# On-chip rotary tables, paired tiles and weights cast in flight in an eight-core encoder kernel

## The chip, the cores and the metric

The kernel runs on all eight cores of one Trainium2 chip. Each core computes two of the sixteen sequences and holds all weights; no core talks to another. The time is the device time of the slowest core in microseconds (us). A core has five engines that run their own instruction streams: TensorE (PE; its weight loads are listed as PEld), VectorE (DVE), ScalarE (ACT), GpSimd (POOL) and SyncE (SP), which here does nothing but issue DMA transfers. Some executions fall into a slower state of the chip, with the cores of one die or of both at a lower clock (in one run of e1, cores 0 to 3 had 0.875 to 0.881 and the time was 2512.55 us). Only fast runs are compared below.

## The reference, cut to what matters

```python
n1 = rmsnorm(h, g_mix)
q, k, v, u, gates = split(n1 @ w_in)
q, k = apply_rope(rmsnorm(q, g_q), cos, sin), apply_rope(rmsnorm(k, g_k), cos, sin)
a = gqa_block_attention(q, k, v) @ w_attn_up          # every key, both directions
p = (multiscale_pool(u) @ pool_w * pool_scale) @ w_pool_up
h = h + (g_a * a + g_p * p) @ w_out                   # sigmoid gates g_a, g_p
n2, mn = rmsnorm(h, g_cross), rmsnorm(mem, g_mem)     # 256 memory tokens a sequence
h = h + softmax((n2 @ w_xq) @ (mn @ w_xk).T / 16) @ (mn @ w_xv) @ w_xo
h = h + square(relu(rmsnorm(h, g_ffn) @ w_ff1)) @ w_ff2
return rmsnorm(h, g_final)                            # x is 16 x 2048 x 1024, f32
```

The kernel works in eight blocks of 512 tokens a core. Before block 0 it makes keys and values of the first sequence (four tiles), and beside the attention of block 0 it folds the memory weights: w_xq with the memory keys, the memory values with w_xo.

## The kernel before

The program is not written in the order in which it runs. Python code builds a graph of operations, and an order-maker, a list scheduler in the same file, walks it with a cost for each operation, chooses an engine where several could do it, gives buffer slots, and writes one fixed sequence for each engine. Its costs are constants in the file:

```python
DMA_BW = 318.0; BACKLOG = 6000.0; DMA_LAT = 2000.0; DMA_ISSUE = 420.0
# a DMA may be placed when its queue is less than BACKLOG behind
if o.dma is not None:
    r = max(r, dma_free - BACKLOG)
...
def pool_t(n):                       # ns of a GpSimd tensor_tensor
    return 150.0 + n * 1.9
def TT(fn, R, W):                    # either engine; the order-maker chooses
    return G.op((("dve", dve_t(512)), ("pool", pool_t(512))), fn, R, W, port=True)
```

A weight is read as f32 in two halves of 128x1024 (on its first one to three uses) and cast to bf16 by one of three engines; from its last such use a bf16 copy goes to a scratch tensor, from which later uses load it. Both stores and loads go through SyncE.

```python
SIZES = dict(W=(10, 2048, BF16), M2=(10, 1024, F32), M1=(24, 512, F32), S1=(70, 512, BF16), KV=(4, 2048, BF16))
wst = nc.dram_tensor("wst", [NU, 2, 128, 1024], F32, kind="ExternalInput").ap()
...
for hf in range(2):                                  # in weight()
    r = V(f"raw{name}{i}{hf}", "M2")
    load(lambda r=r: ap(r), wst[uid, hf], 524288, [r])
    copy_any(lambda w=w, hf=hf: ap(w)[:, hf * 1024:(hf + 1) * 1024], lambda r=r: ap(r), 1024, ...,
             engs=("pool", "act", "dve") if scale is None else ("act", "dve"))
if keep and n == late:
    store(wsc[uid], lambda w=w: ap(w), 524288, [(w, 0), (w, 1)], [dram(("wsc", key))])
...
def rope_tables(tb):                                 # cos and sin of a tile: two loads
    for i in range(2):
        c = V("cs", "M1")
        load(lambda c=c: ap(c), rope_d[tb, i], 262144, [c], early=30000.0)
```

The softmax here doesn't subtract the row's maximum and nothing guards it: scores larger than these inputs give would overflow.

Of the kernel before, what the change touches and what calls it, by code (L numbers as in the profile page):

```python
# [65 lines left out]
DMA_BW = 318.0  # L66
BACKLOG = 6000.0
DMA_LAT = 2000.0
DMA_ISSUE = 420.0
ALT_BIAS = 300.0  # L70
# [132 lines left out]
def schedule(G, pools, horizon, pe_ahead):  # L203
# [75 lines left out]
    while n_left:  # L279
# [4 lines left out]
        for level in range(2):  # L284
            for e in engines:
# [5 lines left out]
                for U, i, o in lst:  # L291
# [11 lines left out]
                    if best is not None and r > best[0] + 400.0 and r > s_min + 400.0:  # L303
                        n += 1
                        continue
# [14 lines left out]
                if best is None or c[0] < best[0]:  # L320
                    best = (c[0], e, c[3])
# [37 lines left out]
        if o.mms is not None:  # L359
            if o.mms[0]["mode"] != last_mode:  # L360
                start += SWITCH
            last_mode = o.mms[-1]["mode"]
            d = o.dur
            o.start, end = start, start + d
            o.finish = end + PE_TAIL
        elif e == "sp":
            end = start + DMA_ISSUE
            dma_free = max(dma_free, end) + o.dma / DMA_BW
            o.start, o.finish = start, dma_free + DMA_LAT
            d = DMA_ISSUE  # L370
        else:
            d = dict(o.engs)[e]
            o.start, end = start, start + d
            o.finish = end
            if e == "pool" or o.port and e == "dve":
                port_free = end
# [30 lines left out]
def emit(nc, stack, order):  # L407
# [33 lines left out]
    for o in allops:  # L441
# [12 lines left out]
        if o.dma is not None:  # L454
            kn = known[e]
            idle = [s for s, c in dcount.items() if kn.get(("d", s), 0) >= 16 * c]
            s = min(idle, key=lambda s: dcount[s]) if idle else len(dcount)
# [16 lines left out]
    dsem = {s: stack.enter_context(nc.semaphore(f"d_{s}")) for s in dcount}  # L474
# [48 lines left out]
def build_core(info=None):  # L523
    nc = bass.Bass("TRN2", target_bir_lowering=False, dynamic_dma_scratch_size=256)
    xT = nc.dram_tensor("xT", [2, 4, 8, 128, 512], F32, kind="ExternalInput").ap()
    memT = nc.dram_tensor("memT", [8, 128, 512], F32, kind="ExternalInput").ap()
    wst = nc.dram_tensor("wst", [NU, 2, 128, 1024], F32, kind="ExternalInput").ap()
    vec_d = nc.dram_tensor("vec", [128, 64], F32, kind="ExternalInput").ap()
    rope_d = nc.dram_tensor("rope", [4, 2, 128, 512], F32, kind="ExternalInput").ap()
    band_d = nc.dram_tensor("band", [2, 128, 864], F32, kind="ExternalInput").ap()  # L530
# [3 lines left out]
    n1d = nc.dram_tensor("n1d", [2, 4, 8, 128, 512], BF16).ap()  # L534
    pdd = nc.dram_tensor("pdd", [2, 4, 4, 128, 512], BF16).ap()
# [3 lines left out]
    with st:  # L539
# [3 lines left out]
        SIZES = dict(W=(10, 2048, BF16), M2=(10, 1024, F32), M1=(24, 512, F32), S1=(70, 512, BF16), KV=(4, 2048, BF16))  # L543
# [9 lines left out]
        poolw = sb("poolw_sb", [128, 512], BF16)  # L553

# [6 lines left out]
        def ap(v):  # L561
            if v.pool == "E":
                return ps[:, v.slot, :]
# [3 lines left out]

        def b16(v):
            return ap(v).bitcast(BF16)

        CONST = {k: Val(k, None) for k in ("vec", "nbg", "ones", "bd", "band", "poolw")}
# [14 lines left out]
        def pool_t(n):  # L586
            return 150.0 + n * 1.9
# [25 lines left out]

        def store(dst, src, nbytes, R, W):
# [21 lines left out]
        def constants():  # L636
            load(lambda: vec[:], vec_d, 32768, [CONST["vec"]])
            for i in range(2):
                b = V("bandraw", "M2")
                load(lambda b=b: ap(b)[:, 0:864], band_d[i], 442368, [b])  # L640
                copy_any(lambda i=i: band[:].rearrange("p a n -> p (a n)")[:, i * 864:(i + 1) * 864],
                         lambda b=b: ap(b)[:, 0:864], 864, [b], [(CONST["band"], i)], psum=False, rate=2.0)
            b = V("pwraw", "M2")
            load(lambda b=b: ap(b)[:, 0:512], poolw_d, 262144, [b])
            copy_any(lambda: poolw[:], lambda b=b: ap(b)[:, 0:512], 512, [b], [CONST["poolw"]], psum=False, rate=2.0)
# [10 lines left out]
        def weight(name, i, keep=True, scale=None):  # L656
# [4 lines left out]
            if key in UNITS and n <= late:  # L661
                uid = UNITS[key]
                for hf in range(2):
                    r = V(f"raw{name}{i}{hf}", "M2")
                    load(lambda r=r: ap(r), wst[uid, hf], 524288, [r])
                    sc = None if scale is None else (lambda hf=hf: vec[:, scale + 2 * i + hf:scale + 2 * i + hf + 1])
                    copy_any(lambda w=w, hf=hf: ap(w)[:, hf * 1024:(hf + 1) * 1024], lambda r=r: ap(r), 1024,
                             [r] + ([CONST["vec"]] if scale is not None else []), [(w, hf)], psum=False, scale=sc, rate=2.0,
                             engs=("pool", "act", "dve") if scale is None else ("act", "dve"))
# [43 lines left out]
        def scaled(h, g, r, name="n"):  # L713
            n = V(name, "S1")
# [7 lines left out]
        def rope_tables(tb):  # L722
            cs = []
            for i in range(2):
                c = V("cs", "M1")
                load(lambda c=c: ap(c), rope_d[tb, i], 262144, [c], early=30000.0)
# [28 lines left out]
        def pool_tile(s, tb):  # L755
            mmsg = []
            for g in range(4):
# [3 lines left out]
                for i, kt in enumerate(kts):  # L761
# [7 lines left out]
                                  i == 0, i == len(kts) - 1, [(u, 0), (u, 1), (CONST["band"], 0), (CONST["band"], 1)],  # L769
                                  n=max(hi - lo, 230)))  # L770
                mmsg.append((g, b, mms))
            for g, b, mms in mmsg:
                PE(mms, [b])
                p = V("pd", "S1")
                copy_any(lambda p=p: ap(p), lambda b=b: ap(b), 512, [b], [p], engs=("act", "dve"))
                if (s, tb) == (0, 0):
                    PD0.append(p)
                else:
                    store(pdd[s, tb, g], lambda p=p: ap(p), 131072, [p], [dram(("pd", s, tb, g))])

        def tile_steps(s, tb, W):
# [3 lines left out]
            def norm():  # L785
# [11 lines left out]
                st_["n"] = [scaled(xs[kc], C_GMIX + kc, r, "n1") for kc in range(8)]  # L797
# [35 lines left out]
            def keep():  # L833
# [3 lines left out]
                for kc in range(8):  # L837
                    n = st_["n"][kc]
                    store(n1d[s, tb, kc], lambda n=n: ap(n), 131072, [n], [dram(("n1", s, tb, kc))])
# [12 lines left out]
        def memory_steps():  # L852
            m = {}

            def norm():
# [10 lines left out]
                m["n"] = [scaled(xs[kc], C_GMEM + kc, r, "mn") for kc in range(8)]  # L866
# [14 lines left out]
            def fold_a(h, ch):  # L881
                def f():
                    if ch == 0:
                        m["wq"] = weight("XQ", h, keep=False)
                        m["A"] = [V("A0", "W"), V("A1", "W")]
                    w, At = m["wq"], m["A"]
                    b = V("fa", "D")
                    PE([mm(lambda: ap(b), wsl(w, dt * 1024 + ch * 128), lambda dt=dt: ap(m[("XK", 2 * h + dt)]), dt == 0, dt == 1,
                           [(w, dt), m[("XK", 2 * h + dt)]]) for dt in range(2)], [b])
                    for s in range(2):  # L890
                        copy_any(lambda s=s: ap(At[s]).rearrange("p (a k d) -> p a k d", a=2, d=128)[:, :, ch, :],
                                 lambda s=s: ap(b)[:, s * 256:(s + 1) * 256].rearrange("p (a d) -> p a d", d=128), 256,
                                 [b, CONST["vec"]], [(At[s], ch)], scale=lambda: vec[:, C_GCROSS + ch:C_GCROSS + ch + 1],
                                 engs=("act", "dve"))
                    if ch == 7:
                        for s in range(2):
                            store(wsc[SCRATCH[(f"A{s}", h)]], lambda s=s, At=At: ap(At[s]), 524288,
                                  [(At[s], k) for k in range(8)], [dram(("wsc", (f"A{s}", h)))])
# [154 lines left out]
        def query_steps(s, tb):  # L1053
            d_ = {}

            def query(c):
                def f():
                    if c == 0:
                        if (s, tb) not in N1:
                            N1[(s, tb)] = []  # L1060
                            for kc in range(8):
                                n = V("n1g", "S1")
                                load(lambda n=n: ap(n), n1d[s, tb, kc], 131072, [n], R=[dram(("n1", s, tb, kc))], early=15000.0)
                                N1[(s, tb)].append(n)
# [38 lines left out]
        def chain_steps(s, tb, lead, nxt):  # L1103
# [3 lines left out]
            def up_step(j):  # L1107
                def f():
                    if j == 0:
                        c_["pd"] = PD0 if (s, tb) == (0, 0) else []  # L1110
                        for g in range(4 if (s, tb) != (0, 0) else 0):
                            p = V("pdl", "S1")
# [382 lines left out]
```

## Time and profile before

| | |
|---|---|
| time, median of 4 runs | 2254.18 us (2251.19 to 2256.78) |
| cores in the profiled run | 2242.3 to 2253.9 us, granted clock 0.986 to 0.990 |
| PE busy on the slowest core | 2140.6 us, 95% |
| a repeating block of 512 tokens | 246 us |

These are lines of the page's part on DMA queues (packets, MB, share of the time of 16 engines) and of its part on DMA issues (count, KB each, median us from issue to landing), for the kernel before.

```profile
q1 hardware_dynamic: 156096, 440.60, 60.7%
...
HBM read 376.57 MB, written 63.96 MB: 195 GB/s over the span
...
M_p<-wst SPq DMA_DIRECT2D x228, 512.0 KB, 9.8
...
M_p<-rope SPq DMA_DIRECT2D x32, 256.0 KB, 10.7
n1d<-S_p SPq DMA_DIRECT2D x56, 128.0 KB, 9.1
```

One queue carries everything. The 228 half weights, 32 rotary tables and 56 small stores are the rows that the change touches.

### The profile page before, as it was taken

To read this page: it belongs to the slowest core of one execution; us is meant where nothing else is said; L and a number is where in the kernel's file an instruction comes from. 1 tells how busy PE (TensorE), PEld (TensorE's weight loads), DVE (VectorE), ACT (ScalarE), POOL (GpSimd) and SP (SyncE) were. 2 spreads that over 40 slices of the span, in tenths; PEclk is the share of its full clock that TensorE was granted. 3 is DMA by queue.
4 is the path that set the end of the run, shared out by engine and by line. 5 is a ranking of instruction groups with operands and counts; after the bars stand their busy time and mean duration, and the time that the engine had idled before them with its cause. 6 is when DMAs were issued, how large, how long until landed. Compare 5 with 4: busy or idle time off the path is not lost.

```text
span 2253.9 us, 33704 instructions; the slowest of 8 cores (2242.3 to 2253.9 us)
## 1 busy us (share of the span) xinstructions
PE 2140.6 (95%) x10758; PEld 900.0 (40%) x10758; DVE 1471.4 (65%) x1793; ACT 1481.2 (66%) x1875; POOL 368.5 (16%) x273
## 2 busy tenths in 40 slices
PE   6788999988999999999999999999999999999997
PEld 3423333333444434444434443444434443444443
DVE  4688876667876687666774578557774687456502
ACT  6678777747786477853788368854786368835550
POOL 0112321124221241101110021002110122000100
PEclk9999999999999999999999999999999999999998
DMA  9957995989587992946633463435533463336342
GB/s 284 287 189 244 299 306 185 286 277 314 199 275 267 284 306 101 299 153 197 211 113 122 151 223 104 139 124 191 174 117 117 168 215 113 123 128 226 127 145 75
DMA packets 156267, 442.75 MB, mean 196 GB/s; under 512 B 17472, under 2 KB 38976, under 8 KB 156096
## 3 DMA queue, kind: packets, MB, share of 16 engines
q1 hardware_dynamic: 156096, 440.60, 60.7%
q8 instruction: 91, 1.49, 0.3%
q14 instruction: 80, 0.66, 0.1%
HBM read 376.57 MB, written 63.96 MB: 195 GB/s over the span
## 4 chain that ended last, share of the span: by engine, by line
PE 81%; DMA 6%; ACT 4%; DVE 4%; issue 3%; SPq 1%; POOL 0%; DVEq 0%; ACTq 0%; POOLq 0%
PE ps L603 81%; DMA M_p<-wst 3%; ACT M_p L1014 2%; DMA wsc<-W_p 1%; SPq L611 1%; DMA outT<-M_p 1%; SPq L615 1%; DMA M_p<-xT 1%; DVE M_p L1270 0%; DMA vec_sb<-vec 0%; ACT M_p L1241 0%; DVE M_p L1025 0%; ACT M_p L709 0%; DVE S_p L715 0%; ACT W_p L623 0%
## 5 line engine op out<-in xcount | busy, mean ns | idle before, releaser
L603 PE MATMUL ps<-S_p,W_p 128*128 128x512 bf16 x7680 | 1731.9, 381 | 33.1 <-DVE S_p L715 7.7
L603 PEld LDWEIGHTS ps<-S_p,W_p 128*128 128x128 bf16 x7680 | 733.7, 98 | 996.2 <-issue 160.3
L1014 ACT ACTIVATE M_p<-ps 128x2048 bf16<-128x2048 f32 x256 | 479.5, 1873 | 220.3 <-PE ps L603 215.9
L1025 DVE TENSOR_TENSOR M_p<-M_p 128x1024 f32<-128x1024 f32 x224 | 284.5, 1270 | 162.2 <-ACT M_p L1014 158.0
L1026 DVE TENSOR_TENSOR M_p<-M_p 128x1024 f32<-128x1024 f32 x224 | 309.6, 1382 | 17.4 <-DVE M_p L1025 0.9
L698 POOL TENSOR_TENSOR M_p<-M_p 128x512 f32<-128x512 f32 x67 | 101.3, 1512 | 806.3 <-ACT M_p L689 710.4
L689 ACT ACTIVATE M_p<-M_p 128x512 f32<-128x512 f32 x216 | 134.1, 625 | 137.2 <-DVE M_p L1222 47.0
L626 POOL CAST W_p<-M_p 128x1024 bf16<-128x1024 f32 x92 | 115.1, 1256 | 493.8 <-PE ps L603 291.8
L1241 ACT ACTIVATE M_p<-ps 128x512 f32<-128x512 f32 x256 | 151.6, 592 | 46.7 <-PE ps L603 45.2
L1257 DVE TENSOR_TENSOR M_p<-ps,M_p 128x512 f32<-128x512 f32 x64 | 44.2, 691 | 208.3 <-PE ps L603 208.3
L603 PE MATMUL ps<-S_p,KV_p 64*128 64x512 bf16 x1024 | 157.1, 385 | 15.4 <-ACT M_p L1014 14.8
L603 PE MATMUL ps<-M_p,KV_p 128*64 128x512 bf16 x1024 | 137.0, 389 | 16.6 <-ACT M_p L1014 12.3
L1245 ACT ACTIVATE S_p<-M_p 128x512 bf16<-128x512 f32 x220 | 138.6, 630 | 20.4
L623 ACT ACTIVATE W_p<-M_p 128x1024 bf16<-128x1024 f32 x71 | 74.4, 1051 | 108.1 <-PE ps L603 88.3
L1092 ACT ACTIVATE M_p<-ps,nbg 128x512 f32<-128x512 f32 x128 | 87.1, 685 | 58.7 <-PE ps L603 57.9
L603 PE MATMUL ps<-W_p,S_p 128*128 128x256 bf16 (+2 forms) x576 | 96.1, 318 | 4.0 <-ACT W_p L623 1.8
L603 PEld LDWEIGHTS ps<-M_p,KV_p 128*64 128x64 bf16 x1024 | 49.3, 110 | 96.7 <-issue 72.2
L626 DVE CAST W_p<-M_p 128x1024 bf16<-128x1024 f32 x61 | 42.7, 716 | 65.4 <-PE ps L603 29.2
L603 PEld LDWEIGHTS ps<-S_p,KV_p 64*128 64x128 bf16 x1024 | 29.6, 94 | 121.4 <-issue 121.3
L603 PE MATMUL ps<-S_p,ones_bf 128*128 128x512 bf16 x166 | 56.5, 403 | 19.0 <-ACT S_p L689 11.6
L603 PEld LDWEIGHTS ps<-W_p,S_p 128*128 128x128 bf16 x576 | 55.1, 100 | 43.6 <-issue 21.3
L1095 ACT ACTIVATE M_p<-M_p 128x1024 f32<-128x1024 f32 x64 | 67.5, 1055 | 4.1
(76 smaller groups left out, 1486.7 us busy)
## 6 DMA issues: line engine op xcount, KB each, us to landing
W_p<-wsc SPq DMA_DIRECT2D x383, 512.0 KB, 4.3
M_p<-wst SPq DMA_DIRECT2D x228, 512.0 KB, 9.8
wsc<-W_p SPq DMA_DIRECT2D x69, 512.0 KB, 9.3
M_p<-xT SPq DMA_DIRECT2D x128, 256.0 KB, 10.6
outT<-M_p SPq DMA_DIRECT2D x64, 256.0 KB, 4.7
M_p<-rope SPq DMA_DIRECT2D x32, 256.0 KB, 10.7
n1d<-S_p SPq DMA_DIRECT2D x56, 128.0 KB, 9.1
S_p<-n1d SPq DMA_DIRECT2D x56, 128.0 KB, 5.6
```

The lines of the kernel that those rows point to most:

```text
L603: return e.matmul(out(), lhsT=lhsT(), rhs=rhs(), start=start, stop=stop, skip_group_check=True, **kw)
L623: return e.activation(out=dst(), in_=src(), func=AF.Copy)
L626: return e.tensor_copy(out=dst(), in_=src())
L689: A(lambda e: e.activation(out=ap(sq), in_=src(), func=AF.Square), 512, False, R, [sq])
L698: TT(lambda e: e.tensor_tensor(out=ap(out), in0=ap(acc), in1=ap(sq), op=ALU.add), [acc, sq], [out])
L1014: A(lambda e: e.activation(out=b16(P).rearrange("p (a n) -> p a n", n=512), in_=ps[:, 0:4, :], func=AF.Exp, scale=0.125), 2048, True, S, [P])
L1025: D(lambda e: e.tensor_tensor(out=ap(acc), in0=ap(acc), in1=lo(), op=ALU.add), 1024, [P, acc], [acc], port=True)
L1026: D(lambda e: e.tensor_tensor(out=ap(acc), in0=ap(acc), in1=hi(), op=ALU.add), 1024, [P, acc], [acc], port=True)
L1092: A(lambda e, b=b, i=i: e.activation(out=ap(Et)[:, i * 512:(i + 1) * 512], in_=ap(b), func=AF.Exp, bias=nbg[:, i * 8 + j:i * 8 + j + 1], s ...
L1095: A(lambda e: e.activation(out=ap(Et), in_=ap(Et), func=AF.Ln, bias=1.0, scale=1.0), 1024, False, [(Et, 0), (Et, 1)], [(Et, 0), (Et, 1)])
L1241: A(lambda e: e.activation(out=ap(rl), in_=ap(b), func=AF.Relu), 512, True, [b], [rl])
L1245: e.activation(out=ap(H), in_=ap(rl), func=AF.Square))
```

## The change

Its intent is to free engines, SyncE and bandwidth in the crowded front of the run. Weights come as one transfer of 1 MB, cast to bf16 on the way and issued by GpSimd; rotary tables are products of a small table in SBUF; n1 and pooled tiles travel in pairs; folding writes 512 columns at a time. With it come new constants of the order-maker. The core of the diff, cut where marked:

```diff
-DMA_BW = 318.0
-BACKLOG = 6000.0
+DMA_BW = 385.0
+DMA_FIX = 200.0
+BACKLOG = 5000.0
+SW_ISSUE = 620.0
+SW_LAT = 3000.0
...                       (SyncE may be placed up to 1600 ns later, not 400, and is preferred when urgent)
-    wst = nc.dram_tensor("wst", [NU, 2, 128, 1024], F32, kind="ExternalInput").ap()
+    wst = nc.dram_tensor("wst", [NU, 128, 2048], F32, kind="ExternalInput").ap()
...
-M1=(24, 512, F32), S1=(70, 512, BF16)
+M1=(32, 512, F32), S1=(50, 512, BF16)
...
         def pool_t(n):
-            return 150.0 + n * 1.9
+            return 270.0 + n * 1.95
...
+        def load_cast(dst, src, nbytes, W):
+            return G.op((("pool", SW_ISSUE + nbytes / DMA_BW + SW_LAT),), lambda e: e.dma_start(out=dst(), in_=src), (), W,
+                        dma=nbytes)
...                                                  (weight)
-                for hf in range(2):
+                if scale is None:
+                    load_cast(lambda w=w: ap(w), wst[uid], 1048576, [(w, 0), (w, 1)])
+                for hf in range(2) if scale is not None else ():
...                                                  (rope_tables)
-                load(lambda c=c: ap(c), rope_d[tb, i], 262144, [c], early=30000.0)
+                TT(lambda e, c=c, i=i: e.tensor_tensor(
+                    out=ap(c).rearrange("p (r c) -> p r c", c=64),
+                    in0=rope[:, i * 32 + tb * 8:i * 32 + tb * 8 + 8].unsqueeze(2).to_broadcast([128, 8, 64]),
+                    in1=rope[:, 64 + i * 64:128 + i * 64].unsqueeze(1).to_broadcast([128, 8, 64]), op=ALU.mult),
...                                                  (n1; the pooled tiles likewise)
-                for kc in range(8):
-                    store(n1d[s, tb, kc], lambda n=n: ap(n), 131072, [n], [dram(("n1", s, tb, kc))])
+                for k2 in range(4):
+                    store(n1d[s, tb, k2], lambda v=v: b16(v), 262144, [(v, 0), (v, 1)], [dram(("n1", s, tb, k2))])
...                                                  (fold_a: four products of 256 columns, one eviction of 512)
-                    for s in range(2):
-                        copy_any(..., 256, [b, CONST["vec"]], [(At[s], ch)], scale=..C_GCROSS.., engs=("act", "dve"))
+                    copy_any(..., 512, [b], [(At[s], c2)], engs=("act", "dve"))
...
-                    rounded(j, None)
+                    rounded(j, C_GCROSS)
```

## The prediction

> **What bounds the kernel now.** I read the per-core list first: cores 2242 to 2254 us, both dies at clock 0.987 to 0.988, so the fast state and no odd core. Then the page's busy line, then a table of busy time by stage whose cuts I chose at the borders that the timeline shows: the four key/value tiles (to 118 us), the folding of the memory weights beside attention block 0 (to 257), the first block (to 560), blocks 1 and 2 with the late tiles (to 1150), three repeating blocks, the end. Columns of the table: stretch, length, busy time of PE, PEld, DVE, ACT, POOL with instruction counts, granted clock, DMA share, GB/s.
>
> ```profile
> PE 2140.6 (95%) x10758; PEld 900.0 (40%) x10758; DVE 1471.4 (65%) x1793; ACT 1481.2 (66%) x1875; POOL 368.5 (16%) x273
> ...
> 0.00:118.00 118.00, 85.20 (x484) 44.16 (x484) 65.91 (x119) 77.56 (x132) 12.85 (x15) 0.92 0.99 285
> 118.00:190.00 72.00, 57.06 (x283) 19.95 (x285) 61.64 (x79) 57.09 (x69) 15.85 (x12) 0.94 0.63 207
> 190.00:257.00 67.00, 59.88 (x307) 21.24 (x304) 56.81 (x63) 51.04 (x55) 11.62 (x9) 0.97 0.79 254
> 257.00:560.00 303.00, 282.49 (x1370) 116.06 (x1369) 220.21 (x266) 218.00 (x266) 86.92 (x66) 0.98 0.88 276
> 560.00:1150.00 590.00, 579.30 (x3031) 251.07 (x3031) 424.85 (x522) 404.48 (x515) 117.75 (x89) 1.00 0.70 225
> 1150.00:1396.00 246.00, 242.94 (x1216) 99.48 (x1210) 160.43 (x184) 162.44 (x198) 33.17 (x22) 1.00 0.45 150
> ```
>
> The reader is to see two kernels in one. From 1150 us on a block takes 246 us, PE is busy for 242.9 of them and DMA for 45%: nothing that feeds PE matters there. PE's idle time sits at the front: 118 - 85.2 = 32.8 us, then 14.9, 7.1, 20.5 and 10.7. If PE idled throughout at the rate of a repeating block (3.1 of 246), the first 1150 us would hold 14 us of idle; they hold 86. About 72 us is thus the whole prize, and some 18 of it is the start, before the first projection matmul at 18.3 us. Each early stage has its own limit: DMA to 118 us (share 0.99), DVE and ACT from 118 to 190 (61.6 and 57.1 of 72), DMA and casts mixed after that.
>
> The timeline around 80 to 101 us shows the front's worst hole (start, duration, engine, line, instruction, in brackets the idle time before and what ended it):
>
> ```profile
> 79.29 7.42 SPq L615 DMA_DIRECT2D n1d<-S_p  x8
> ...
> 86.75 1.40 SPq L611 DMA_DIRECT2D M_p<-wst  x2
> ...
> 98.72 1.06 ACT L623 ACTIVATE W_p<-M_p 128x1024 bf16<-128x1024 f32 x1 [7.22 <-DMA M_p<-wst]
> ...
> 100.89 1.18 PE L603 MATMUL ps<-S_p,bd_bf 128*128 128x512 bf16 x2 [5.28 <-ACT S_p L732]
> ```
>
> Eight small stores hold the SP queue for 7.4 us, the weight load behind them lands at 98.6, its cast follows, and PE has idled 5.3 us.
>
> **What the Trainium skill says.** (1) "DMA: Bandwidth & Descriptors", section "SWDGE vs HWDGE vs iDMA": a DMA that changes the type has to come from GpSimd, whose cores write the descriptors in software. The kernel before has no such DMA, so no row shows the cost. (2) Same page, "Issuing engines are not separate DMA queues": transfers from all engines share the same 16 DMA engines, so a second issuer saves issue time, not bandwidth. The trace agrees with the premise: with one issuer the DMA share is already 0.99 at 285 GB/s. (3) "SBUF — State Buffer", section "Who interferes with whom": a DVE instruction in a 2-port mode locks GpSimd out of its SBUF port, and descriptor writing waits. The trace has candidates (DVE casts 1024 f32 in 716 ns, hardly more than the 691 of its undisturbed sum of two 512 wide operands, so a fast mode) but they are short, and 61 of them disappear. (4) DMA page, "Rules for kernel authors": small transfers pay mostly overhead, coalesce. Here a 128 KB n1 store lands in 9.1 us and a 512 KB scratch load in 4.3, but the former run in the crowded part, so this is weak support.
>
> **The change part by part.**
>
> ```profile
> L626 POOL CAST W_p<-M_p 128x1024 bf16<-128x1024 f32 x92 | 115.1, 1256 | 493.8 <-PE ps L603 291.8 <-DMA M_p<-wst 181.7 <-DMA wsc<-W_p 20.1
> ...
> L623 ACT ACTIVATE W_p<-M_p 128x1024 bf16<-128x1024 f32 x71 | 74.4, 1051 | 108.1 <-PE ps L603 88.3 <-DMA M_p<-wst 18.1 <-DMA wsc<-W_p 1.7
> ...
> L626 DVE CAST W_p<-M_p 128x1024 bf16<-128x1024 f32 x61 | 42.7, 716 | 65.4 <-PE ps L603 29.2 <-DMA M_p<-wst 28.8 <-DMA wsc<-W_p 7.2
> ...
> L627 DVE TENSOR_SCALAR W_p<-ps,vec_sb 128x256 bf16<-128x256 f32 x33 | 14.7, 478 | 3.9 <-PE ps L603 2.0 <-DMA wsc<-W_p 1.3
> ...
> L624 ACT ACTIVATE W_p<-ps,vec_sb 128x256 bf16<-128x256 f32 x31 | 13.3, 476 | 3.6 <-DVE W_p L627 1.5 <-DMA wsc<-W_p 1.2 <-PE ps L603 0.4
> ```
>
> Casts: 92 + 71 + 61 = 224 go, worth 115 us of POOL, 74 of ACT, 43 of DVE (four scaled halves stay). None lies after 1150 us. In their place POOL issues 112 transfers of 1 MB; at an assumed 1 us each (my estimate, near an SP issue of 0.3 to 0.9 us) POOL keeps about the same load as before. HBM reads stay the same, only the SBUF side is halved. SP issues fall from 1084 to about 740.
>
> Rotary tables: 32 loads of 256 KB go (8.4 MB, 1.9% of all bytes); ten of them are issued before 118 us, 2.6 MB, at 285 GB/s 9 us of DMA time where DMA is the limit. Added: 32 products of 128x512 f32, about 0.69 us on DVE (that form, undisturbed) or 1.3 to 1.5 on POOL: 22 to 45 us over the whole run, 7 us of it in the first stage, hidden beside DMA.
>
> Pairing: n1 and pooled stores and loads fall from 168 to 84, same bytes. It halves holes like that at 79 us, 4 us each at most, and overlaps with the gain from weights leaving the SP queue.
>
> Folding: 64 evictions of 128x256 (28.0 us of DVE and ACT) become 32 of 128x512, at 684 (DVE) or 601 ns (ACT) about 20.6 us: 7.4 saved. But 64 matmuls of 512 columns become 128 of 256. In the tiles 16 such took 2.34 us (146 ns each), 16 of 512 columns 3.63 (227 each): 64 x (2 x 146 - 227) = 4 us more PE time. The gain g_cross moves into the rounding of h: 18 casts of 832 ns leave POOL for ACT or DVE (706 or 600 ns), some 16 us spread over all blocks, hidden.
>
> The sum by stage. To 118 us: 9 us less DMA time; the first matmul cannot start much sooner (vec, x and three weight units must land), so I give it 8. From 118 to 257: ACT and DVE lose 11.6 + 4.3 us of casts and 7.4 of evictions, 23 in all, 11.6 each when shared; 2 us of table products and 4 of PE time come back, and attention's chain of score, exponential, sum does not shrink: I give it 8 of the 22 us idle. From 257 to 560: 1 MB of tables at 276 GB/s is 3.8 us, and 56 us of casts leave ACT and DVE; of 20.5 us idle I give it 7. To 1150: 2. After: 0. Sum 25, less 1 for dearer rounding between stages: 24, so 2255.9 - 24 = 2232 us.
>
> **The rivals.** (a) The buffer takes the place of the cast. Before, the raw half sat ready in its own buffer, and when a weight slot came free only a cast of about 1 us lay between; now a slot must be free before the load starts, and loads take 7 to 12 us to land in the front. The chain of waits already has the scratch store as the freeing event (5.5 us at 178, 7.9 at 237). Against it: ten slots, and a weight is used up in about 3.6 us (16 matmuls), so 36 us of lead, against some 10 + 4 + 9 for load, use and store. If it binds, it eats the gain of the middle stages: 2250 to 2275. (b) POOL becomes a gate: its instructions run in order, so a transfer stands behind a sum that waits for ACT. POOL is 11 to 29% busy in the front, which speaks against it; 0 to +15 us. (c) DMA stays the limit and the casts were hidden anyway: then only the removed table bytes count, some 9 + 4 us, 2243. (d) All of it works and PE idles as in a repeating block except for the start: 72 - 18 = 54 us, 2202. That is the floor of what I believe.
>
> **Range and chances.** Over 2% faster needs less than 2211, 45 of the 54 us in (d): 0.15. Slower by over 2% needs 2301; no row offers 45 us of new wait unless (a) and (b) meet: 0.05. Range 2204 to 2258, (d) at its low end and a mild (a) at the other.
>
> **What would show each step.** The repeating blocks should still take 246 us; if they shrink, my reading of the bound is wrong. No casts of 128x1024 f32 into W_p but four, no table loads, SP issues near 740. PE idle to the end of the tiles near 25 instead of 33, in the folding stage near 14 instead of 22, in the first block near 14 instead of 20. Rival (a) would show as matmuls waiting directly on weight DMA with the issue waiting on a scratch store, (b) as POOL's issues late behind its sums, (c) as the same DMA share of 0.99 and an unchanged length of the middle stages. What would make it wrong most likely: cast transfers that run faster or slower per byte than plain ones, which nothing here shows, or a changed order of instructions that moves idle time by itself.

## The result, and the profile after

The changed kernel takes 2277.76 us, the median of four runs (2272.62 to 2310.91, the last of them slow). The kernel before, on the same chip, takes 2254.18. The ratio of fast runs is 1.0097, with a 95% interval from 1.0073 to 1.0122. (Ratios here and below are the mean time of one kernel's fast runs over the mean of the other's fast runs of the same rounds, so they are not quite the ratio of the medians.) The change is within 2%, on the slow side, and outside my range.

The page of the changed kernel, its slowest core:

```profile
PE 2145.9 (94%) x10822; PEld 907.9 (40%) x10822; DVE 1409.2 (62%) x1702; ACT 1428.8 (63%) x1819; POOL 339.5 (15%) x307
...
q1 hardware_dynamic: 106848, 313.70, 41.2%
q0 software_dynamic: 16416, 59.30, 16.9%
...
L627 POOL DMA_DIRECT2D W_p<-wst x112 | 60.8, 544 | 519.6 <-PE ps L615 424.5
...
W_p<-wst POOLq DMA_DIRECT2D x112, 512.0 KB, 8.7
```

The parts do what was meant. DVE and ACT each lose over 50 us of work, a second queue carries 112 cast transfers (the page counts the 59 MB that they write), and POOL spends 544 ns on each. A cast transfer lands 8.7 us after its issue. PE has 64 more matmuls and 5 us more work. The table by stage, for the slowest core (5), has the columns of the one in the prediction (its cuts are points in time, so the two kernels need not be at the same piece of work there):

```profile
0.00:118.00 118.00, 80.86 (x480) 43.41 (x480) 70.75 (x118) 66.28 (x126) 23.99 (x30) 0.94 0.92 221
118.00:190.00 72.00, 60.88 (x370) 27.60 (x368) 54.48 (x59) 49.73 (x49) 6.88 (x11) 0.92 0.54 124
190.00:257.00 67.00, 59.02 (x289) 20.30 (x287) 46.39 (x51) 45.49 (x48) 4.76 (x9) 0.95 0.82 189
257.00:560.00 303.00, 277.94 (x1357) 113.52 (x1357) 187.80 (x230) 189.59 (x237) 67.82 (x76) 0.98 0.84 185
560.00:1150.00 590.00, 568.87 (x2923) 245.14 (x2924) 397.53 (x490) 380.87 (x490) 106.45 (x95) 0.98 0.66 186
1150.00:1396.00 246.00, 243.45 (x1218) 100.19 (x1216) 161.04 (x185) 163.90 (x199) 32.44 (x21) 1.00 0.45 149
```

PE's idle time is the length of a stage less its first entry: 37.1, 11.1, 8.0, 25.1 and 21.1 us to 1150 us, 102.4 in all. Before, the same sum was 86.1. So 16.3 us of new idle time and 5.3 of new work make 21.6 of the 22.4 us between the two slowest cores (2276.3 and 2253.9). DMA is busier than before only from 190 to 257 us (0.82 for 0.79), so the new idle time is not a plain lack of bandwidth.

The same loss can be read by blocks, and then it has a place. I take the last product of a block's final norm, on DVE, as the block's end, read from the timeline of each of the eight cores of the profiled runs:

| | block 0 ends at | block 1 takes | block 2 takes |
|---|---|---|---|
| before | 514 to 520 us (mean 518.0) | 274 to 280 (276.6) | 270 to 274 (271.4) |
| changed | 499 to 512 us (mean 506.0) | 283 to 302 (291.1) | 274 to 282 (277.9) |

So a gain of 12 us is there at the end of block 0, and blocks 1 and 2 lose 14.5 and 6.5 us. In block 1 it is mostly idle time: on the cores without missing records PE runs 1376 to 1380 matmuls there (before 1381 to 1384) and idles 13 to 25 us (before 6 to 11). In block 2 it is mostly work that was put off: PE runs 1424 matmuls there (before 1403) and idles about as long as before.

The list of cores shows something that an average hides. The first four of eight:

```profile
core 0: 2269.5 us, clock 0.985
core 1: 2241.1 us, clock 0.991
core 2: 2263.3 us, clock 0.988
core 3: 2238.3 us, clock 0.990
```

One core of each neighbouring pair is some 25 us later than the other, and that other is as fast as before or faster; in another run of the same kernel the other one of a pair was late. In the profiled run of the kernel before, the two of a pair were 7 to 11 us apart. The mean over the cores rose from 2247.3 to 2255.9 only; the slowest core sets the time.

The largest single loss of the slow core is seen at the border of blocks 0 and 1. First SyncE's issues there in the kernel before (core 3), then in the changed one (core 5), with start, duration, what they move and count; then the two longest pieces there of the changed kernel's chain of waits (start, duration, what), and a matmul of its PE, with the idle time before it in brackets:

```profile
512.26 4.41 SPq L611 DMA_DIRECT2D M_p<-xT  x7
516.76 7.60 SPq L615 DMA_DIRECT2D outT<-M_p  x8
524.42 0.44 SPq L611 DMA_DIRECT2D M_p<-xT  x1
```

```profile
504.21 2.73 SPq L623 DMA_DIRECT2D M_p<-xT  x5
507.55 5.86 SPq L631 DMA_DIRECT2D outT<-M_p  x8
521.28 11.35 SPq L623 DMA_DIRECT2D M_p<-xT  x3
```

```profile
511.52 19.33 DMA outT<-M_p
...
530.91 10.40 DMA M_p<-xT
```

```profile
546.24 7.36 PE L615 MATMUL ps<-M_p,W_p 128*128 128x512 bf16 x20 [11.07 <-ACT M_p L1110]
```

The kernel before asks for seven of the next block's eight x tiles ahead of the output stores. The changed one asks for five; the other three take buffers that an output store must leave first. The chain of waits of the changed kernel has that store for 19.33 us from 511.52 and then the x load for 10.40 us. The exponential of a gate on ACT comes behind it, and PE stands for 11 us. Its 20 matmuls after the hole take 7.36 us, 368 ns each, where sixteen of the same form before the hole took 3.61 us, 226 each. So this hole cost 2.8 us more than its own length. Holes of 8 to 13 us stand at this border on two of the four late cores here, on three in e10 and on all four in e5 and e9, and on no early core; in the kernel before and in e12 PE waits there for 2.1 and 3.1 us at most.

### The profile page after: what moved, and what is told of

It reads as the page before. It is cut to its first block, busy times and chain, and to the rows that moved or that the text cites. A ratio compares the mean times of both kernels' runs of the same rounds, so it can differ in the third digit from the quotient of the medians.

```text
span 2276.3 us, 32739 instructions; the slowest of 8 cores (2238.3 to 2276.3 us)
## 1 busy us (share of the span) xinstructions
PE 2145.9 (94%) x10822; PEld 907.9 (40%) x10822; DVE 1409.2 (62%) x1702; ACT 1428.8 (63%) x1819; POOL 339.5 (15%) x307
## 4 chain that ended last, share of the span: by engine, by line
PE 81%; DMA 9%; DVE 4%; ACT 3%; issue 2%; SPq 0%; DVEq 0%; ACTq 0%; POOLq 0%
PE ps L615 81%; DMA W_p<-wst 3%; DMA M_p<-xT 2%; DMA wsc<-W_p 1%; ACT M_p L1032 1%; DMA outT<-M_p 1%; DVE M_p L726 1%; DMA M_p<-wst 1%; DVE M_p L1287 1%; DMA pdd<-M_p 1%; DVE M_p L1044 0%; DVE M_p L1043 0%; ACT M_p L721 0%; SPq L623 0%; DMA M_p<-n1d 0%
## 5 line engine op out<-in xcount | busy, mean ns | idle before, releaser
L615 PE MATMUL ps<-S_p,W_p 128*128 128x512 bf16 (+1 forms) x6144 | 1375.3, 379 | 26.2 <-DMA W_p<-wst 10.0
L615 PEld LDWEIGHTS ps<-S_p,W_p 128*128 128x128 bf16 x6144 | 586.2, 98 | 783.4 <-issue 122.9
L615 PE MATMUL ps<-M_p,W_p 128*128 128x512 bf16 x1600 | 384.5, 389 | 26.2 <-ACT M_p L1110 11.1
L615 PEld LDWEIGHTS ps<-M_p,W_p 128*128 128x128 bf16 x1600 | 154.4, 99 | 234.5 <-issue 67.2
L710 POOL TENSOR_TENSOR M_p<-M_p 128x512 f32<-128x512 f32 x73 | 112.0, 1536 | 799.4 <-ACT M_p L701 749.0
L615 PE MATMUL ps<-M_p,KV_p 128*64 128x512 bf16 x1024 | 137.9, 391 | 16.4 <-ACT M_p L1032 6.2
L627 POOL DMA_DIRECT2D W_p<-wst x112 | 60.8, 544 | 519.6 <-PE ps L615 424.5
L615 PE MATMUL ps<-W_p,M_p 128*128 128x384 bf16 (+1 forms) x512 | 76.8, 304 | 1.1 <-DVE M_p L751 0.8
L1261 DVE TENSOR_TENSOR S_p<-ps,M_p 128x512 bf16<-128x512 f32 x36 | 24.8, 690 | 75.8 <-ACT M_p L1258 75.7
```

What stands on the lines that cost most here:

```text
L615: return e.matmul(out(), lhsT=lhsT(), rhs=rhs(), start=start, stop=stop, skip_group_check=True, **kw)
L627: return G.op((("pool", SW_ISSUE + nbytes / DMA_BW + SW_LAT),), lambda e: e.dma_start(out=dst(), in_=src), (), W, dma=nbytes)
L710: TT(lambda e: e.tensor_tensor(out=ap(out), in0=ap(acc), in1=ap(sq), op=ALU.add), [acc, sq], [out])
```

## The experiments

Eighteen runs of seventeen kernels were made, in six groups; kernels of a group shared a chip and the runs of the kernel before. All gave correct results. In some texts T1 stands for the turnover of weight slots, T4 for the idea that the two cores of a pair slow each other in memory, T5 for the crowded start, and T6 for the pairing. By "front" I mean the end of the first FFN product of block 0, seen on ACT; it comes at 424 to 431 us before and 415 to 426 after.

### Group 1: the cast alone, all but the cast, the order, the reads

**e1**: the changed kernel with weights as halves and casts again.

```diff
-                if scale is None:
-                    load_cast(lambda w=w: ap(w), wst[uid], 1048576, [(w, 0), (w, 1)])
+                for hf in range(2):
+                    load(lambda r=r: ap(r), wst[uid][:, hf * 1024:(hf + 1) * 1024], 524288, [r])
+                    copy_any(...)
```

> The changed kernel with one part undone: first-use weights again as two plain 512 KB loads from SP into a raw buffer and a cast on an engine. Theory T1 (the cast transfer needs a free weight slot before it starts, so the freeing of a slot plus a whole load lies on PE's path, which costs the blocks with many first-use weights): block 1 back from 283-302 us to about 275, block 2 to about 271, no direct wait of PE on a weight load above 1 us, end near 2240. Rival T2 (the order-maker's new constants make loads too late, whoever carries them): block 1 stays at 285-300 and the end near 2275. Rival T3 (pool sizes and pairing, M1 and S1): also stays near 2275.

Ratio 1.0161 (1.0099 to 1.0224), fastest run 2277.5 us, from two fast runs; front 432 to 442 us, later than before. Taking the cast out does not bring the time back. By blocks it moves the loss: block 1 is back at 275 us in the mean of the cores, as T1 expected, but block 0 ends at 532 us and not at 506. This run already said that something besides the cast costs time.

**e2**: the kernel before with cast transfers (and, because one transfer takes a whole weight, the new layout of wst).

> The kernel before with one part of the change alone: first-use weights by 1 MB cast transfers from GpSimd into the weight slot, old constants, old pools, tables loaded. T1: block 1 grows from 277 to 285-300 us, the cores of a pair part by 20 us or more, end 2265-2285. T2 and T3: block 1 stays within 5 us of 277, end at or below 2255.

Ratio 1.0181 (1.0121 to 1.0242). The order put the first key weights late: the first projection matmul came at 44 to 46 us (before: 16 to 18). So it tells more of that order than of the cast, and two things changed at once.

**e3**: the changed kernel with the old constants of the order-maker (DMA_BW 318, DMA_FIX 0, BACKLOG 6000, the old thresholds for SyncE).

> The changed kernel with the order-maker's constants and SP preference of before (assumed bandwidth 318, no fixed cost, backlog 6000, old thresholds); work and buffers as in the change. T2: block 1 back to about 277 us and end near 2240-2250. T1: block 1 stays at 285-300 us and end 2265-2285.

Ratio 1.0109 (1.0077 to 1.0140). Taking the new DMA constants out gains nothing. But the order that the old ones make puts the first projection matmul at 54 to 56 us, as e2's does, so this run too shows an order and not the constants alone.

**e4**: the changed kernel, every weight read as f32 once only (LATE = 0 for all but the key weights).

> The changed kernel with each weight read as f32 once only, in block 0, and from the bf16 scratch after that; 64 fewer MB-sized cast transfers in blocks 1 and 2, all scratch stores in block 0. T1: blocks 1 and 2 drop to 265-272 us, block 0 grows by 10-25 us for its stores, the end 2240-2275. T2: block 1 changes by less than 8 us.

The two fast runs took 2269.0 and 2269.2 us, the median of the kernel before beside them was 2248.1. Block 1 shortens to 266 us from 291 (mean of the cores), but block 0 ends at 525 to 543 us rather than 499 to 512. Time moves from one block to the other. (The cast transfers fell from 112 to 70, by 42 and not by the 64 of the text.)

### Group 2: slots, start, preference

**e5** and **e6**: weight slots 12 and 9 rather than 10.

```diff
-W=(10, 2048, BF16), M2=(10, 1024, F32)
+W=(12, 2048, BF16), M2=(8, 1024, F32)        # e5;  e6: W=(9, ...), M2=(10, ...)
```

> The changed kernel with 12 weight slots in place of 10 and 8 two-KB-wide f32 slots in place of 10, same bytes. T1 (a cast transfer needs a free slot before it starts, so PE waits on loads where slots turn over slowly): from the end of the first FFN product in block 0 to the end of block 1, 369-389 us on the eight cores of the changed kernel, falls to 355-368 and the cores of a pair come within 10 us; end near 2250. Rival T4 ([...]slots don't matter): that stretch stays at 369-389 and pairs stay 25 us apart.

> The changed kernel with 9 weight slots, nothing else changed. T1: the same stretch grows by 8 to 20 us, and PE's direct waits on weight transfers grow; end 2285-2300. T4: within 5 us of the changed kernel.

Ratios 1.0082 (1.0064 to 1.0099) and 1.0107 (1.0086 to 1.0129); the pairs of cores of e5 are as far apart as those of the changed kernel. Between 9 and 12 slots lies 0.25%, within the intervals, and block 1 still takes 286 and 289 us in the mean of the cores. So a shortage of slots, my rival (a), is not what costs most of the time.

**e7**: the three key and value weights plain through SyncE, all others cast.

```diff
-                if scale is None:
+                if scale is None and key[0] != "KV":
```

> The changed kernel with only the key/value weight units (three at the start, three for each late tile) by plain loads from SP and a cast on an engine. Theory T5 (three 1 MB casts on a second queue share the DMA engines with the first x tile, which comes 8 us later than before): first projection matmul at 18 us in place of 25.7, the fourth tile's norm some 5 us sooner than 73, end 5 to 8 us sooner than the changed kernel, 2268 or so. If the late start is absorbed by the DMA limit of the first 118 us, the first projection moves but the norm of the fourth tile and the end don't.

The first projection matmul comes at 18.6 to 19.4 us rather than 25.5 to 26.1, as expected, and the front is no earlier (422 to 434 us); ratio 1.0128 (1.0106 to 1.0150). The changed kernel's late start is real, and undoing it gains nothing that is left at the front.

**e8**: the changed kernel with the new DMA constants but the old thresholds for SyncE.

> The changed kernel with the order-maker's old SP thresholds (no preference for urgent SP transfers, old look-ahead of 400 ns), its assumed bandwidths as in the change. If the preference makes the hole at the border of blocks 1 and 2 (end of block 1 to the last up-projection of block 2: 32 us before, 36 us in the change, 31 with all old constants), that stretch falls to 31-33 us here; if the assumed bandwidths and backlog make it, it stays at 36.

One fast run, 2278.3 us, the others slow; no ratio. Nothing speaks for the preference, but the first projection matmul comes at 54 to 56 us here too, so it is a weak test; the stretch that the text names I did not read.

### Group 3: the pairing

**e9** takes the pairing out of the changed kernel (n1 and pooled tiles singly in S1, M1 24, S1 66). **e10** keeps it and gives M1 36 slots for 32 (M2 8). **e11** is the kernel before with the pairing alone:

```diff
-M1=(24, 512, F32), S1=(70, 512, BF16)
+M1=(32, 512, F32), S1=(50, 512, BF16)
-n1d = nc.dram_tensor("n1d", [2, 4, 8, 128, 512], BF16).ap()      # pdd likewise
+n1d = nc.dram_tensor("n1d", [2, 4, 4, 128, 1024], BF16).ap()
```

> The changed kernel with the pairing undone: n1 and pooled tiles back in the 1 KB slots, stored and loaded singly, pools 24 f32 and 66 bf16 slots (same bytes). Theory T6 (paired n1 and pooled tiles fill the f32 slots, so at a block's border the next block's x loads wait on SP until the last block's output stores have landed): SP's waits on output stores at the border of blocks 0 and 1 fall from 16.7 us to below 3, PE's hole there of 3.8 to 11 us goes, the stretch from the first FFN product of block 0 to the last up-projection of block 1 is 125-129 us on all cores (127-139 in the change), cores of a pair within 12 us, end 2252-2262. Rival T4 (two cores of a pair starve each other in memory whatever the slots): stretch and pair difference stay as in the change, end 2270-2280.

> The changed kernel with 36 f32 slots of 2 KB in place of 32, paid for by 8 in place of 10 of 4 KB. T6: the hole at the border of blocks 0 and 1 shrinks on all cores, stretch 125-131 us, end 2255-2265. T4: no change, 2270-2280.

> The kernel before with the pairing alone (n1 and pooled tiles in f32 slots, 32 and 50 slots as in the change), plain weight loads, loaded tables, old constants. T6: x loads wait on output stores at block borders, the stretch from first FFN product of block 0 to last up-projection of block 1 grows from 127 to 131-139, end 2258-2275. If pairing is harmless by itself: 127 and end at or below 2255.

Ratios 1.0074 (1.0021 to 1.0127), 1.0084 (1.0002 to 1.0167) and 0.9957 (0.9872 to 1.0042). Taking the pairing out of the changed kernel gains nothing clear: the order still puts five x loads ahead of the output stores, the hole at the border stays (12.4 us on core 5), and block 1 takes 293 us. So the hole does not come from the pairing, and T6 is not the cause. Alone the pairing seems to help: front at 415 to 420 us, though the interval of e11 takes in no change at all. A part of the change was good, and the good kernel gave a base to which parts could be added one by one.

### Group 4: what is bad without the cast, and the second queue

**e12** is the changed kernel with plain weights and old order constants (the edits of e1 and e3 together). **e13** differs from e12 in the issuer alone: GpSimd issues the plain halves, the engines cast them.

```diff
-                    load(lambda r=r: ap(r), wst[uid][:, hf * 1024:(hf + 1) * 1024], 524288, [r])
+                    load_cast(lambda r=r: ap(r), wst[uid][:, hf * 1024:(hf + 1) * 1024], 524288, [r])   # f32 to f32
```

**e14** is the changed kernel with SW_LAT 12000 for 3000, so that its order counts on later landings. **e15** repeats e11.

> Kernel after with weights by plain loads from SyncE and casts on the engines, and with the order-maker's old constants: what stays of the change is the rotary tables made on chip, the pairing and the new fold. If cast transfers and the new constants are the two harms: 2235 to 2250 us, its cores within 20 us of each other, first FFN product of block 0 at 415 to 425 us. If tables or fold do the harm: 2260 us or more, although pairing alone measured 2242.

> As the kernel before it in this job, but the plain f32 loads of the weights are issued by GpSimd on its own queue instead of SyncE; casts stay on the engines. It holds the second queue without the casting. If the second queue (its share of the DMA engines) is the harm: 20 us or more above its twin, cores of a pair 20 to 30 us apart, first projection product after 22 us. If casting in the transfer is the harm: within 8 us of its twin, cores together.

> Kernel after with one constant of the order-maker changed: it takes 12 us instead of 3 us between the end of a cast transfer's bytes and its landing (measured landing 8.7 us median), so it places the scratch stores of SyncE later and the first products of a fresh weight too. If SyncE's waits on landings, with x, outT and n1 transfers behind them, are the harm: wait of SyncE on W_p<-wst falls from 324 us to under 120 us, and the time to 2255 or less. If the shared DMA engines are: waits fall but the time stays at 2265 to 2280 and the cores of a pair stay apart.

> Pairing alone again, since its first measurement had few fast runs: 2235 to 2250 us, ratio to the kernel before under 1.000. If the first result was chance: ratio 1.00 to 1.005.

e12: 2279.85 us, ratio 1.0105 (1.0089 to 1.0121). It has no cast transfers of weights and is as slow as the changed kernel, against what I expected. e3 is the same kernel with cast transfers, at 1.0109. In the total the cast in flight is worth nothing measurable here. But the orders differ (the first projection matmul comes at 19 to 20 us in e12 and at 54 to 56 in e3), and the two lose in different blocks, as the second table of the ladder shows.

e13: 2303.76 us, ratio 1.0205 (1.0190 to 1.0220), 1.0% above e12. Moving the same transfers to GpSimd costs that much before any casting, together with the new order that it brings (eight x loads ahead of the output stores, five in e12), and from e13 to e3, which casts in flight on that queue, it is gained back. (e3 ran in another group; each ratio is to the kernel before beside it.) The page of e13 shows that GpSimd now has both to do:

```profile
L626 POOL DMA_DIRECT2D M_p<-wst x224 | 123.3, 553 | 220.5 <-DVE W_p L641 63.3
```

Its first projection matmul came at 30 to 34 us and its pairs of cores were 11 to 13 us apart, not the 20 to 30 expected. So the second queue by itself does not part the pairs that far.

e14: SyncE's waits on landings fell from 324 to 208 us, not to under 120 as the test needed, and the time rose to 2291.92, ratio 1.0157 (1.0143 to 1.0172). The order changed with the constant (first projection matmul at 29 to 30 us). That SyncE waits in order on cast landings is thus not shown to be the cause, nor ruled out.

e15: 2247.41 us, ratio 0.9956 (0.9943 to 0.9969). The pairing alone is a real gain of 0.4%.

### Group 5: the fold, and all but the fold

**e16** adds the new fold to e15. **e17** is e12 with the old fold.

> Kernel before with the pairing and the new fold (four products of 256 columns and one eviction of 512 in place of two and two, the gain moved to the rounding of the hidden state); tables, loads, casts and order-maker as in before. If the fold is what takes back the gain: 2260 to 2280 us, the first FFN product of block 0 at 430 us or later (pairing alone 413 to 420). If the fold is the gain that I predicted: 2235 to 2247 us.

> The kernel of e12 with the fold of before: pairing, tables made on chip, constants by cast transfer, new rate of GpSimd in the order-maker; plain weights, old order-maker constants. If the fold is the harm in e12 (2280 us): 2240 to 2255 us, first FFN product at 413 to 425 us. If tables, constants or GpSimd's rate are: 2265 us or more, first FFN product at 430 us or later.

e16: 2246.35 us, ratio 0.9984 (0.9963 to 1.0006), front 412 to 420. e17: median 2273.66 us, ratio 1.0117 (1.0086 to 1.0148), front 423 to 445. The fold is cleared of a large loss: e17 without it is as slow. That it costs some us is not ruled out, since e16 lies 0.0028 above e15 and their intervals only just overlap. What is left in e17 is guilty of e17's loss.

### Group 6: the tables, without layout and rate

**e18** is e15 plus tables made on chip and constants by cast transfer. It differs from e17 in two edits only:

```diff
-    wst = nc.dram_tensor("wst", [NU, 128, 2048], F32, kind="ExternalInput").ap()     # e17
+    wst = nc.dram_tensor("wst", [NU, 2, 128, 1024], F32, kind="ExternalInput").ap()  # e18
-            return 270.0 + n * 1.95                                                  # pool_t
+            return 150.0 + n * 1.9
```

> The kernel of e15 (pairing alone) plus tables made on chip and constants by cast transfer; weights plain from two contiguous halves, GpSimd's rate in the order-maker and everything else as before. It differs from e17 (2274 us) only in the stored layout of the weights and that rate. If making the tables on chip (or loading the constants by cast) is the harm: 2265 us or more, first FFN product of block 0 at 423 us or later, its cores over 20 us apart, as e17. If the layout or the rate is: 2238 to 2252 us, first FFN product at 412 to 421 us, cores within 20 us.

2241.93 us (2240.12 to 2243.66, five runs), ratio 0.9967 (0.9953 to 0.9981), cores 2228.6 to 2240.4, front 410 to 417. Tables and constants are cleared. This is the fastest median of all kernels and beats both the kernel before and the changed one; by ratio e15 is level with it. Here are the first four stages of e17 (core 1) and of e18 (core 1):

```profile
0.00:118.00 118.00, 88.90 (x516) 45.94 (x517) 79.95 (x129) 80.74 (x133) 29.16 (x28) 0.96 0.97 288
118.00:190.00 72.00, 57.95 (x293) 19.78 (x290) 62.18 (x71) 59.12 (x74) 21.20 (x15) 0.95 0.52 163
190.00:257.00 67.00, 53.40 (x261) 18.24 (x260) 51.57 (x55) 48.68 (x51) 11.19 (x9) 0.92 0.86 236
257.00:560.00 303.00, 282.34 (x1365) 115.82 (x1363) 216.28 (x259) 215.51 (x267) 86.89 (x65) 0.98 0.87 270
```

```profile
0.00:118.00 118.00, 91.55 (x537) 47.49 (x538) 81.03 (x135) 85.98 (x140) 31.18 (x30) 0.96 0.98 299
118.00:190.00 72.00, 59.41 (x309) 21.26 (x308) 62.62 (x76) 58.01 (x70) 16.82 (x12) 0.98 0.58 170
190.00:257.00 67.00, 55.56 (x269) 19.80 (x268) 53.73 (x63) 48.63 (x56) 16.17 (x13) 0.95 0.86 275
257.00:560.00 303.00, 287.93 (x1409) 118.68 (x1407) 226.27 (x269) 223.74 (x272) 87.37 (x67) 0.98 0.86 280
```

To 560 us the PE of e18 has idled 26.5 + 12.6 + 11.4 + 15.1 = 65.6 us and that of e17 77.4, and e18 has by then issued 2524 matmuls to 2435. That is 12 us more idle time to 560 us, where the two cores are 29 us apart at the end, and no stage holds most of it.

### The ladder

Read in this order the runs lead from the kernel before to the changed one, one part more in each row. Every ratio is to the kernel before on the same chip.

| kernel | ratio | 95% interval | run |
|---|---|---|---|
| before, with the pairing | 0.9956 | 0.9943 to 0.9969 | e15 |
| and tables on chip, constants by cast | 0.9967 | 0.9953 to 0.9981 | e18 |
| and the layout of wst and GpSimd's rate | 1.0117 | 1.0086 to 1.0148 | e17 |
| and the fold | 1.0105 | 1.0089 to 1.0121 | e12 |
| and weights cast in flight, from GpSimd | 1.0109 | 1.0077 to 1.0140 | e3 |
| and the new DMA constants: the changed kernel | 1.0097 | 1.0073 to 1.0122 | result |

One step stands out: 0.0150 of 2250 us, 34 us. The totals of all others lie within their intervals of nothing, but for the pairing, a gain of 10 us. But a total can hide two changes that cancel. The same rows by blocks, means of the eight cores of each profiled run:

| run | block 0 ends at | block 1 takes | block 2 takes |
|---|---|---|---|
| before | 518.0 | 276.6 | 271.4 |
| e15 | 508.5 | 274.3 | 273.4 |
| e18 | 507.7 | 269.4 | 276.9 |
| e17 | 523.1 | 279.6 | 275.6 |
| e12 | 531.3 | 277.1 | 275.8 |
| e3 | 524.6 | 287.6 | 271.6 |
| changed kernel | 506.0 | 291.1 | 277.9 |

The step of 34 us is a loss of 15 us in block 0 and 10 in block 1. The changed kernel does not have that loss in block 0: with the cast in flight and the new DMA constants block 0 is as early as in the good kernels, and block 1 is 14 us longer than in e12. Over all runs the kernels that load first-use weights by cast transfer in block 1 need 283 to 293 us for it in the mean of the cores (e14 alone 277, and it loses in blocks 0 and 2), and those that load them plainly through SyncE 269 to 280 (e13, plainly through GpSimd, 279); e4, which has few such transfers left there (four after 510 us on core 5, the changed kernel 41), needs 266. So casting in flight is not without effect, and what the changed kernel loses is not simply the step of 34 us carried along. How much it would gain by the old rate and layout is not known: no run has the changed kernel without them.

### What stays open

I have no run with the layout alone or the rate alone, and none with cast transfers beside the pairing and the old rate. Two things bear on which of the two lines it is. For bandwidth, I divided the bytes of SyncE's queue by the time it was busy on each core: 331 GB/s in the mean of the cores in e18, 323 in e17; but 326 in e15 and 325 in e12, which has the new layout and is 32 us slower than e15 on the same chip. The queue has the same 139104 packets and 431.16 MB in e17 and e18. So a slower transfer does not explain it by itself. For the order: the layout does not enter the order-maker at all, while the rate does, and the instruction listings of e17 and e18 differ from about 30 us on. At the border of blocks 0 and 1 the fast kernels (before, e11, e15, e16, e18) had seven x loads ahead of the output stores; of the others most had four to six, and e4 and e13 eight. That speaks for the order, and it is an argument, not a test: the number is a mark of the order rather than the cause, since e12, with five, has no hole there above 3.1 us. If it is the rate, the new one is not a worse estimate: for 512 columns the old formula gives 1123 ns and the new one 1268, and the 67 sums of the profile before took 1512 in the mean. Why the cores of a pair part by 25 us is open too, and T4 was not tested. In the profiled runs the widest pair of a kernel with the contiguous layout was 11 us apart, that of a kernel with the new one 13 to 31, but only 10 in e2.

## Why the prediction was wrong, point by point

**The bound was read rightly.** The repeating blocks take 245.5 us, PE-bound as before. Four scaled casts are left, no table loads, and 742 issues on SyncE (the prediction said 740).

**The step that failed is the sum by stage**, "From 118 to 257 ... I give it 8", "From 257 to 560 ... I give it 7" and "To 1150: 2". It turned freed time of ACT and DVE into time of PE. The freed time is there, 62 us of DVE and 52 of ACT. PE idle in those three stages is 19.1, 25.1 and 21.1 us, where I said 14 and 14 for the first two and had 22.1, 20.5 and 10.7 before. By blocks, block 0 ends 12 us sooner, a part of it by putting work off, and the term "To 1150: 2" turned into a loss: blocks 1 and 2 take 21 us more, in the mean of the cores. On the slow core PE waits 11 us at the border of blocks 0 and 1 and some 7 us on cast transfers in block 1, and no term of the sum had such waits. Why they come is known in part: they come with the cast transfers, and the number of slots hardly changes them. The sum also started from an unspoken premise, that the order of instructions would stay as good as it was. The prediction's last sentence names "a changed order of instructions that moves idle time by itself" and puts no time on it. The largest step of the ladder, 34 us, comes with two lines that I had priced at nothing, GpSimd's rate and the layout. That this is also what the changed kernel lost is likely in part and not shown.

**"To 118 us I give it 8"** failed as well. The slow core idles 37.1 us there, not 25. The prediction said that the first matmul "cannot start much sooner"; it starts 8 us later, at 25.5 to 26.1, because 3 MB of key weights on the second queue now share the DMA engines with the first x tile: on core 5 its last piece lands at 22.1 us, and at 14.6 in e7, where these weights come through SyncE behind it. e7 takes this back and gains nothing by the front. The 9 us of table bytes bought nothing that shows: e18 is no faster than e15.

**The pairing was mis-sized.** I gave it "4 us each at most" and no term of its own. It measured 10 us (e15) and is the one part that clearly pays.

**The fold** adds 64 matmuls as I said. PE's work rose by 5.3 us (I had 4), but it differs as much between kernels without the fold (2145.3 us in e15, 2134.3 in e18), so its price is not settled. It gained nothing that e16 or e12 shows, and may cost a little (e16).

**The rivals.** (a) is seen, as PE waiting directly on a cast transfer, for 12.1 us in ten waits on the slow core, some 7 of them in block 1; but neither 9 nor 12 slots moved the time much. It named 2250 to 2275 us for the case that it binds, which is nearly what was measured, for another reason than the slots. (b) is not the way it went in the changed kernel: POOL is 15% busy and needs 544 ns for an issue, half my estimate; in e13, where it also casts, 1.0% is lost. The lock of GpSimd's port, point (3), does not show in the issues, which took 527 to 714 ns. (c) had the right core, that the casts were hidden anyway, though not for its reason: DMA's share to 118 us fell to 0.92. (d) never came near.

**The range** of 2204 to 2258 had its upper end at a "mild (a)". It had no room for a worse order, nor for (a) at its own price.

## What to carry to other kernels

When a scheduler writes the order, a change of one of its cost constants is a change of the kernel: run it alone, before the parts that look important. A saving on engines off the critical path is worth what the waits behind it are worth, so look for the wait it ends, not for the busy time it frees. When a bundle disappoints, build it up from the good kernel part by part; of the first ten runs nine took parts out of the bad one or turned its knobs, and told me little. And compare block by block before comparing totals: e12 and the changed kernel have the same ratio and lose in different blocks.

## What the Trainium skill lacked or had wrong

- "DMA: Bandwidth & Descriptors", section "SWDGE vs HWDGE vs iDMA", says that each DMA engine alternates between the queues that the two kinds of issuer feed. It does not say what that costs a mixed program. Here 3 MB on the second queue put the first projection matmul at 25.5 to 26.1 us rather than 18.6 to 19.4 (e7), and moving plain loads to that queue, with the order that came of it, cost 1.0% (e13 against e12).
- The same page, section "Anatomy of one DMA — SWDGE (gpsimd) path", fits 2.0 us plus the bytes at 436 GB/s, which makes 4.4 us for 1 MB (my estimate from that page). Beside this kernel's other traffic the cast transfers of 1 MB took 5.1 to 16.4 us from issue to landing, 8.7 in the median. That does not show the fit to be wrong, since no run has such a transfer alone; the section lacks what other traffic adds.
- No page has it that neighbouring cores with the same program can end 25 us apart, the late one changing from run to run (24 to 29 us in the profiled run of the changed kernel, 7 to 11 in that of the one before).
